# Spatial half's norm summed over one addend, and the first weight's three loads issued by ScalarE's queue

## The chip, the cores and the metric

The kernel runs on one core of a Trainium2 chip. Its engines, as the profile names them, are PE (TensorE: matmuls, with PEld for the loading of the stationary operand), DVE (VectorE), ACT (ScalarE), POOL (GpSimd) and SP (SyncE, which here only issues loads and stores). Each engine works through its own instructions in their written order and waits on semaphores for the others. Loads and stores are moved by 16 DMA engines; an instruction on SP, ACT or POOL issues one, and the transfer then runs beside the engines.

The metric is the device time of one execution in microseconds (us). The kernel before took 1024.92 us, the median of three runs (1023.53 to 1025.2).

## The reference

One decoder layer on 512 tokens of 1024 features, in float32: a SwiGLU feed-forward block, a mixing sub-layer, a second SwiGLU block, a gated per-layer embedding and a last norm. The change touches the embedding's product, which the kernel computes first, and the norm of the mixing sub-layer's spatial half:

```
def rmsnorm(x, g):
    xf = x.astype(jnp.float32)
    y = xf * lax.rsqrt(jnp.mean(xf * xf, axis=-1, keepdims=True) + EPS)
    return (y * g.astype(jnp.float32)).astype(x.dtype)

        ya = chunked_spatial_gating(jax.nn.gelu(u, approximate=False), jax.nn.gelu(v, approximate=False),
                                    gm_ln_g[i], gm_ln_b[i], gm_w_s[i], gm_b_s[i])
        ya = rmsnorm(ya, gm_out_norm[i])
        yb = mamba2_mixer(z, xbc, dt_raw, conv_w[i], conv_b[i], dt_bias[i], a_log[i], d_skip[i], ssm_norm[i])
        h = h + jnp.concatenate([ya, yb], axis=-1) @ w_out[i]
    ...
        gate = jax.nn.sigmoid(rmsnorm(h, ple_norm[i]) @ ple_w_gate[i] + ple_b_gate[i])
        h = h + gate * (p[i] @ ple_w_proj[i])
```

## The kernel before, in words

Features lie on the 128 partitions and tokens along a row, so a tile of 128 features by 512 tokens is the unit of work. Every large product is made of three matmuls: each factor is split into a rounded high part (`hi`, a cast by ACT) and a remainder (`lo`, a subtraction by DVE), and `hi*hi`, `hi*lo` and `lo*hi` are added up in an accumulator bank. So each weight that arrives by DMA passes ACT and then DVE before PE can use it whole.

The program is a list of steps, each with a product on PE, a load, a split and follow-up work. A planner (`run`) issues the steps' parts in turn. For the first steps, up to step 14, the order is written out by hand in the table `ENTRY` (tokens such as `load0`, `split0`, `product0`). The order on PE, ACT, DVE and SP is the written one.

**The entry.** Step 0 is `embedding(0)` (L1187 to L1244 of the kernel before). Its `load` (L1199 to L1203) issues on SP, in this order: the first half of the embedding `p` into the tile `g`; the first weight `ple_proj[0]` into a `raw` tile, in three pieces of 256, 256 and 512 columns (L1202); and the second half of `p` (L1203). Behind them on SP come the second weight `ple_proj[1]` (512 KB, L512), the vector of gains `vec`, the first four tiles of the activations `h` (L1269), the feed-forward weights (`raw`, `rawb`, L512), and the rows of x for the first norm (`whix`, `wlox`, L384). A load waits for an earlier load on the same semaphore, and there are eight of these, used in turn; so from the eighth load or so each one waits for an earlier one to have landed. The split of step 0 (L1215 to L1221) casts the first half of `p` and the first two pieces on ACT and DVE, and then the second half of `p` with the third piece. Its product (L1231) is 24 matmuls of 512 columns, first twelve from the first half and then twelve from the second.

Before that product, PE runs seven matmuls on zeros (L174), and ACT runs one copy of a single column (L175), whose only use is that ACT's function table is loaded there.

**The spatial half's norm.** In the mixing sub-layer the eight tiles `u[i]` are multiplied by their gates on DVE (L1833, `mix_times_u`). For the norm over all features the squares are needed, summed over tiles and partitions. An object `gn` of the class `Norm` squares the first seven tiles on ACT and adds them on POOL into one tile, `ssum` (L276 to L280). The eighth square (L1838) is kept apart in `mix["sq"]`, a tile called `tmp`. The method `sums` (L299 to L311) then sums over partitions with matmuls of one column against a tile of ones (L307): for each of four chunks of 128 tokens one with `ssum` and one with the last square, both into the same column. PE does this behind the product of the second output step (`out_steps[1].rest`); DVE then forms the factor per token (L240 to L246), spreads it over a diagonal (L331), and PE multiplies that by ones (L344).

## Time and profile before

| | us |
|---|---|
| median of three runs | 1024.92 |
| the profiled execution | 1026.13 |
| its span, first to last instruction | 1024.1 |
| PE busy in the span | 1009.1 |
| DVE busy | 843.8 |
| ACT busy | 581.0 |
| first matmul of the embedding starts at | 4.97 |
| second weight `ple_proj[1]` lands at | 9.41 |
| spatial half's norm: its first matmul of one column starts at | 574.73 |

A row of the timeline gives start and duration in us, the engine, the line, the operation with output and inputs, the shapes, a count, and in brackets the idle time ahead of it and what ended it. A row of the chain of waits gives start, duration and what the end of the program waited for in that time. A row of the table by stretches gives, for each engine, its busy time and in brackets its instructions, then the granted clock of PE, the mean busy share of the 16 DMA engines, and what they moved in GB/s. The granted clock of PE was 0.995 over the span.

### The profile page before, as it was taken

How to read it: one execution, taken by the hardware profiler on the slowest of the kernel's cores; microseconds unless marked ns; L12 is line 12 of the kernel's file. 1: busy time of each engine (PE TensorE's matmuls, PEld its weight loads, DVE VectorE, ACT ScalarE, POOL GpSimd, SP SyncE). 2: the span in 40 equal slices, each digit the busy share in tenths (PEclk: the TensorE clock that was granted, in tenths of full speed). 3: DMA queues.
4: the chain of work that ended last, by engine and by line, in shares of the span. 5: the costliest groups of instructions: out<-in, count | busy, mean ns of one | idle time of the engine just before them, and what ended most of it. 6: DMA issues, size and time to landing. Idle time of an engine off the chain costs nothing.

```text
span 1024.1 us, 18334 instructions
## 1 busy us (share of the span) xinstructions
PE 1009.1 (99%) x7472; PEld 951.9 (93%) x7472; DVE 843.8 (82%) x1111; ACT 581.0 (57%) x781; POOL 134.1 (13%) x141
## 2 busy tenths in 40 slices
PE   9999999999999999999999999999999999999996
PEld 7899999999999799888888888899999999999996
DVE  6988888879988797776998757778888888988985
ACT  6755545457667374575754434455445456666745
POOL 0101001002311000144333000101010000330101
PEclk9999999999999999999999999999999999999998
DMA  8977678649962233454432334837677656994412
GB/s 337 325 206 198 192 206 197 195 149 226 207 160 73 82 116 97 148 154 131 137 111 83 103 103 142 215 116 190 183 213 204 176 167 209 217 207 141 136 62 83
DMA packets 51188, 168.89 MB, mean 165 GB/s; under 512 B 5792, under 2 KB 6304, under 8 KB 51104
## 3 DMA queue, kind: packets, MB, share of 16 engines
q1 hardware_dynamic: 39440, 125.71, 36.3%
q0 software_dynamic: 11520, 41.95, 22.1%
q8 instruction: 58, 0.95, 0.4%
q14 instruction: 26, 0.21, 0.1%
q10 hardware_dynamic: 144, 0.07, 0.0%
HBM read 163.44 MB, written 4.26 MB: 164 GB/s over the span
## 4 chain that ended last, share of the span: by engine, by line
PE 85%; DVE 8%; DMA 3%; ACT 2%; issue 1%; SPq 0%; ACTq 0%; DVEq 0%
PE mm L754 20%; PE a L754 15%; PE a L1140 8%; PE sm L217 6%; PE mm L231 6%; PE mm L1140 5%; PE sm L1140 5%; PE mm L217 5%; PE a L217 4%; PE sm L231 3%; PE a L231 3%; DVE wlo L542 2%; DMA s<-in_ffn_gu 1%; PE sm L848 1%; DMA wlox<-in_x_rows 1%
## 5 line engine op out<-in xcount | busy, mean ns | idle before, releaser
L542 DVE TENSOR_TENSOR wlo<-raw,whi 128x1024 fp32r<-128x1024 f32 (+2 forms) x162 | 199.3, 1231 | 66.0 <-ACT whi L538 65.8
L538 ACT CAST whi<-raw 128x1024 fp32r<-128x1024 f32 (+2 forms) x162 | 166.3, 1032 | 139.8 <-DVE raw L764 30.9
L754 PE MATMUL mm<-xfb,whi 128*128 128x256 f32 x960 | 163.9, 275 | 0.0
L754 PEld LDWEIGHTS mm<-xfb,whi 128*128 128x128 f32 x960 | 145.9, 192 | 0.0
L754 PE MATMUL mm<-xfb,wlo 128*128 128x256 f32 x480 | 132.1, 275 | 0.6 <-DVE wlo L542 0.6
L538 ACT CAST whi<-rawb 128x1024 fp32r<-128x1024 f32 x76 | 79.7, 1049 | 62.8 <-DVE rawb L764 29.5
L542 DVE TENSOR_TENSOR wlo<-rawb,whi 128x1024 fp32r<-128x1024 f32 x76 | 92.7, 1220 | 21.3 <-ACT whi L538 20.5
L754 PE MATMUL a<-xfb,whi 128*128 128x256 f32 x640 | 109.4, 275 | 0.0
L754 PEld LDWEIGHTS a<-xfb,whi 128*128 128x128 f32 x640 | 97.3, 192 | 0.0
L754 PEld LDWEIGHTS mm<-xfb,wlo 128*128 128x128 f32 x480 | 92.2, 192 | 0.8 <-DVE wlo L542 0.8
L754 PE MATMUL a<-xfb,wlo 128*128 128x256 f32 x320 | 88.1, 275 | 0.0
L1140 PE MATMUL a<-xfb,whi 128*128 128x256 f32 x480 | 80.7, 275 | 0.0
L1140 PEld LDWEIGHTS a<-xfb,whi 128*128 128x128 f32 x480 | 72.8, 192 | 0.0
L769 POOL DMA_DIRECT2D raw<-in_ffn_gu x20 | 17.2, 862 | 401.7 <-DVE G L916 116.9
L217 PE MATMUL sm<-x,whi 128*128 128x512 f32 x224 | 69.7, 393 | 0.0
L1140 PE MATMUL a<-xfb,wlo 128*128 128x256 f32 x240 | 66.0, 275 | 0.0
L912 ACT ACTIVATE G<-G 128x512 f32<-128x512 f32 x40 | 25.3, 634 | 66.5 <-DVE G L910 65.3
L754 PEld LDWEIGHTS a<-xfb,wlo 128*128 128x128 f32 x320 | 61.4, 192 | 0.1
L754 PE MATMUL a<-xfa,whi 128*128 128x256 f32 x320 | 54.7, 275 | 0.1
L754 PE MATMUL mm<-xfa,whi 128*128 128x256 f32 x320 | 54.8, 275 | 0.0
L1140 PE MATMUL mm<-xfb,whi 128*128 128x256 f32 x320 | 53.8, 275 | 0.0
L1140 PE MATMUL sm<-xfb,whi 128*128 128x256 f32 x320 | 53.8, 275 | 0.0
(430 smaller groups left out, 2612.9 us busy)
## 6 DMA issues: line engine op xcount, KB each, us to landing
raw<-in_ffn_gu SPq DMA_DIRECT2D x56, 512.0 KB, 5.0
rawb<-in_ffn_gu SPq DMA_DIRECT2D x32, 512.0 KB, 8.5
raw<-in_w_in SPq DMA_DIRECT2D x28, 512.0 KB, 3.6
s<-in_ffn_gu SPq DMA_DIRECT2D x20, 512.0 KB, 5.6
raw<-in_ffn_gu POOLq DMA_DIRECT2D x20, 512.0 KB, 6.0
s<-in_ffn_gu POOLq DMA_DIRECT2D x20, 512.0 KB, 9.5
rawb<-in_ffn_dw POOLq DMA_DIRECT2D x18, 512.0 KB, 8.1
raw<-in_w_out SPq DMA_DIRECT2D x16, 512.0 KB, 3.3
```

Of the source, the lines that this page charges most:

```text
L217: nc.tensor.matmul(ps, w, turned(x), start=first and n == 0, stop=last and n == 2, skip_group_check=True)
L231: nc.tensor.matmul(ps[:, tok], wt[:, c], turned(xt[:, tok]), start=first and k == i == 0, stop=last and k == len(xs) - 1 and i == len(by_p ...
L538: nc.scalar.copy(self.hi[:, c], self.raw[:, c])
L542: nc.vector.tensor_tensor(self.lo[:, c], self.raw[:, c], self.hi[:, c].bitcast(F32), ALU.subtract)
L754: nc.tensor.matmul(o, wt[:, c], turned(xt), start=fresh and p == m == n == 0, stop=last and n == 2, skip_group_check=True,)
L769: nc.gpsimd.dma_start(w21.raw, self.src[0], accum_op=ALU.add)
L848: nc.tensor.matmul(ps, (whi, whi, wlo)[n][:, c], t[:, 0:2, n % 2].rearrange("p s (b i) -> p s i b", b=2), start=not lower and p == n == 0, ...
L912: nc.scalar.activation(t, t, AF.Silu)
L1140: nc.tensor.matmul(o, wt[:, c], xt, start=i in (1, 7) and t == jj == n == d % 2 == 0, stop=t == nt - 1 and jj == 1 and d % 2 == 1 and n == ...
```

## The change: what it does

There are two independent parts.

1. The three pieces of the first weight are issued on ACT's queue instead of SP's. ACT's one-column copy, and with it the table load, is moved from ahead of everything to behind these three issues.
2. The eighth square of the spatial half's norm is added to the total by DVE. `sums` loses its second addend, so four matmuls of one column remain where there were eight.

```
-    nc.scalar.copy(vec_warm, ones[:, 0:1])
...
-        def sums(self, more=None):
+        def sums(self):
 
             t = self.totals[0]
             for other in self.totals[1:]:
                 nc.vector.tensor_tensor(t, t, other, ALU.add)
             ps = sm_ps()
             for c in range(NC):
-                for part in (t,) if more is None else (t, more):
-                    nc.tensor.matmul(
-                        ps[:, c : c + 1], part[:, c * P : (c + 1) * P], ones[:, 0:1],
-                        start=part is t, stop=part is not t or more is None,
-                    )
+                nc.tensor.matmul(
+                    ps[:, c : c + 1], t[:, c * P : (c + 1) * P], ones[:, 0:1], start=True, stop=True
+                )
             return ps
...
             for c in halves + (slice(T, 2 * T),):
-                nc.sync.dma_start(w.raw[:, c], a["ple_proj"][q][:, c])
+                nc.scalar.dma_start(w.raw[:, c], a["ple_proj"][q][:, c])
             nc.sync.dma_start(raw[:, 1], a["p"][:, 1])
+            nc.scalar.copy(vec_warm, ones[:, 0:1])
...
         nc.vector.tensor_tensor(u[i], u[i], mix["t", i], ALU.mult)
-        if i < ND - 1:
-            gn.add(u[i])
-        else:
-            mix["sq"] = tmp()
-            nc.scalar.activation(mix["sq"], u[i], AF.Square)
+        if i == ND - 1:
+            gn.engines = (nc.vector,)
+        gn.add(u[i])
...
-    out_steps[1].rest = lambda: gm.update(ps=gn.sums(mix["sq"]))
+    out_steps[1].rest = lambda: gm.update(ps=gn.sums())
```

What stands on the engines is shown at two places. First the start of SP, before; `g` is the embedding's tile, `raw_120` the first weight, `raw_125` the second, `vec` the gains, `h` the activations:

```order
1 L1199 DMA g_98<-in_p 128x512
2 L1202 DMA raw_120<-in_ple_proj 128x256 x2
3 L1202 DMA raw_120<-in_ple_proj 128x512
4 L1203 DMA g_98<-in_p 128x512
5 L512 DMA raw_125<-in_ple_proj 128x1024
6 L1197 DMA vec_69<-in_vecs 128x180
7 L1269 DMA h_94<-in_x 128x512 x2
```

And SP now (line numbers are those of the changed kernel):

```order
1 L1196 DMA g_97<-in_p 128x512
2 L1200 DMA g_97<-in_p 128x512
3 L509 DMA raw_125<-in_ple_proj 128x1024
4 L1194 DMA vec_69<-in_vecs 128x180
5 L1267 DMA h_93<-in_x 128x512 x2
6 L1267 DMA h_94<-in_x 128x512 x2
```

Everything on SP behind the first load stands three issues further forward. The same place on ACT, before; `ghi` and `whi` are the casts of `p` and of the first weight:

```order
1 L175 ACT_TABLE_LOAD
2 L175 COPY warm_75<-ones_76 128x1
3 L1215 CAST ghi_144<-g_98 128x512
4 L1217 CAST whi_146<-raw_120 128x256
5 L1217 CAST whi_146<-raw_120 128x512
```

And ACT now:

```order
1 L1199 DMA raw_119<-in_ple_proj 128x256 x2
2 L1199 DMA raw_119<-in_ple_proj 128x512
3 L1201 ACT_TABLE_LOAD
4 L1201 COPY warm_75<-ones_76 128x1
5 L1213 CAST ghi_144<-g_97 128x512
6 L1215 CAST whi_146<-raw_119 128x256
```

The three issues stand ahead of the table load; the casts keep their order. The second place is DVE at the last tile of the spatial half, before; `u` is the tile, `wlo` the remainder of an output weight, `nv` the first instruction of the norm's factor:

```order
612 L542 TENSOR_TENSOR wlo_6247<-raw_5962,whi_6246 128x1024
613 L1833 TENSOR_TENSOR u_6241<-u_6241,tmp_6244 128x512
614 L542 TENSOR_TENSOR wlo_6281<-raw_6026,whi_6280 128x1024
615 L542 TENSOR_TENSOR wlo_6321<-raw_6102,whi_6320 128x1024
616 L240 TENSOR_SCALAR nv_6325<-sm_6284 128x4
```

And DVE now:

```order
612 L539 TENSOR_TENSOR wlo_6247<-raw_5962,whi_6246 128x1024
613 L1831 TENSOR_TENSOR u_6241<-u_6241,tmp_6244 128x512
614 L279 TENSOR_TENSOR ssum_5950<-ssum_5950,tmp_6251 128x512
615 L539 TENSOR_TENSOR wlo_6282<-raw_6026,whi_6281 128x1024
616 L539 TENSOR_TENSOR wlo_6318<-raw_6102,whi_6317 128x1024
```

The addition into `ssum` stands between the gating of the last tile and the remainders of two output weights; on PE the pairs of L307 (`ssum`, then `tmp`) become four matmuls with `ssum` alone.

## The prediction

> **What bounds the kernel now.** I read the page first, then the chain of waits of the first 60 us, PE's own waits in the timeline, and last the stretch around the spatial half's norm.

> ```profile
> span 1024.1 us, 18334 instructions
> PE 1009.1 (99%) x7472; PEld 951.9 (93%) x7472; DVE 843.8 (82%) x1111; ACT 581.0 (57%) x781; POOL 134.1 (13%) x141
> ```

> PE is busy for 1009.1 of 1024.1 us. So two things can shorten the program: taking work off PE, or filling the few holes in it. The change tries one of each. The holes that matter to its first part are all in the entry:

> ```profile
> 8.69 0.92 PE L1231 MATMUL sm<-ghi,whi 128*128 128x512 f32 x3 [0.33 <-ACT ghi L1219]
> ...
> 27.64 0.70 PE L848 MATMUL sm<-xfb,whi 128*128 128x512 f32 x2 [0.46 <-ACT whi L538]
> 28.89 0.48 PE L848 MATMUL sm<-xfb,wlo 128*128 128x512 f32 x1 [0.56 <-DVE wlo L542]
> 45.75 0.38 PE L754 MATMUL mm<-xfb,wlo 128*128 128x256 f32 x1 [0.61 <-DVE wlo L542]
> ```

> Four stalls, 0.33 + 0.46 + 0.56 + 0.61 = 1.96 us. The chain of waits says what is behind the last of them:

> ```profile
> 0.81 0.38 SPq L1199
> ...
> 1.25 0.42 SPq L1202
> ...
> 1.72 0.42 SPq L1202
> ...
> 2.19 0.43 SPq L1202
> ...
> 2.66 0.43 SPq L1203
> ...
> 3.13 6.28 DMA raw<-in_ple_proj
> ...
> 9.43 6.19 DMA h<-in_x
> ...
> 15.63 9.84 DMA wlox<-in_x_rows
> ...
> 33.18 10.67 DMA s<-in_ffn_gu
> ...
> 45.75 2.72 PE mm L754 x22
> ```

> Up to 45.75 us the end of the program does not hang on PE but on SP's queue: five issues, then the second weight's load (3.13 to 9.41), then a load of `h` that waits for it, then one of the norm's rows, some work of ACT and DVE, and a load of `s`. From 45.75 on the chain is PE's own work. A shift of this chain therefore moves the end of the program, as long as PE's work ahead of 45.75 can move with it, and that has the 1.96 us of stalls to give up.

> **Part 1: three issues leave SP.** The second weight's issue stands at 3.13. The three issues at L1202 take from 1.25 to 2.66, so without them it goes out 2.66 - 1.25 = 1.41 us sooner, at 1.72. That is the upper end for a shift by issue alone. Whether the landings follow is another question, since the load took 6.28 us where loads of this size elsewhere land sooner:

> ```profile
> raw<-in_w_in SPq DMA_DIRECT2D x28, 512.0 KB, 3.6
> ```

> Much of the 6.28 us is spent behind the loads ahead of it. The table by stretches shows how full the 16 DMA engines were:

> ```profile
> 2.00:5.00 3.00, 3.00 (x8) 1.87 (x7) 0.43 (x2) 1.02 (x4) 0.00 (x0) 1.00 0.85 270
> 5.00:7.00 2.00, 2.00 (x8) 1.71 (x8) 1.15 (x2) 0.91 (x2) 0.00 (x0) 1.00 0.58 184
> 7.00:8.00 1.00, 1.00 (x7) 0.85 (x5) 0.00 (x0) 0.00 (x0) 0.00 (x0) 1.00 0.97 349
> 8.00:46.00 38.00, 36.04 (x188) 30.95 (x187) 34.17 (x56) 29.33 (x43) 1.92 (x2) 1.00 1.04 380
> ```

> From 8 to 46 us they are full: nothing can be gained there, but whatever is moved earlier is passed on unchanged, because the same bytes then end earlier. Before 8 us they were idle for 3 x 0.15 + 2 x 0.42 + 0.03 = 1.3 us. So two different bounds agree: 1.41 us of issue, 1.3 us of idle DMA time. The lower bound is zero: from 5 to 7 us the engines were only 0.58 busy although the second weight had been issued at 3.13, so something besides the issue held the loads back, and that may stay. A second queue gives the engines other loads to take up meanwhile. I take 1.0 us, about three quarters of the idle time, nearer to the upper bounds because both the issue and the overlap of queues work the same way; for the likeliest case I allow 0.5 to 1.2.

> [...]

> What does ACT pay? Its rows at the start, and the only load or store that it issues in this program:

> ```profile
> 0.81 1.28 ACT L175 ACT_TABLE_LOAD   x1 [0.81 <-PEq L2177]
> 1.66 3.35 PE L174 MATMUL sm<-tmp 128*128 128x512 f32 x7 [1.66 <-DVE tmp L171]
> 4.21 0.62 ACT L1215 CAST ghi<-g 128x512 fp32r<-128x512 f32 x1 [1.92 <-DMA g<-in_p]
> 4.97 1.44 PE L1231 MATMUL sm<-ghi,whi 128*128 128x512 f32 x3
> 6.19 0.63 ACT L1217 CAST whi<-raw 128x512 fp32r<-128x512 f32 x1 [0.91 <-DMA raw<-in_ple_proj]
> 8.01 0.62 ACT L1219 CAST ghi<-g 128x512 fp32r<-128x512 f32 x1 [1.20 <-DMA g<-in_p]
> ...
> 394.12 0.67 ACTq L1497 DMA_DIRECT2D cs_dram<-csrow  x1
> ```

> ACT is free from the table load's end (2.09, and a copy of 0.2) until the first half of `p` lands at 4.21. Three issues at SP's price (0.43 and a gap of 0.04 each) end at 2.2, the table load then at 3.5, the copy at 3.7: hidden. At ACT's own price of 0.67 they end at 2.9, the table load at 4.2, the copy at 4.4: the first cast is 0.2 us late. Queued behind it are the casts for the first twelve matmuls; PE waits for them, but PE is held by its seven matmuls on zeros until 5.0 in any case, and it has the stall at 8.69 to make up for a late start. That stall ends sooner, since the second half of `p` (cast at 8.01) is issued 1.41 us earlier. The pieces themselves go out at 0.81, 1.5 and 2.2 by ACT's price, against 1.25, 1.72 and 2.19: none is later. I book nothing for ACT; without the cover it is 0.2 us of the 1.96.

> [...]

> **Part 2: four matmuls less, one addition more.** The rows around the norm, then the row for additions of this shape on DVE:

> ```profile
> 542.55 1.05 PE L307 MATMUL sm<-ones,ssum 128*128 128x1 f32 x8
> 543.47 1.14 PE L1819 MATMUL a<-xs,ya 128*128 128x128 f32 x8
> ...
> 568.93 1.27 POOL L280 TENSOR_TENSOR ssum<-ssum,tmp 128x512 f32<-128x512 f32 x1 [5.41 <-ACT tmp L279]
> 571.51 0.68 DVE L1833 TENSOR_TENSOR u<-u,tmp 128x512 f32<-128x512 f32 x1
> 572.28 0.63 ACT L1838 ACTIVATE tmp<-u 128x512 f32<-128x512 f32 x1 [1.95 <-DVE u L1833]
> 573.88 1.23 DVE L542 TENSOR_TENSOR wlo<-raw,whi 128x1024 fp32r<-128x1024 f32 x1 [1.69 <-ACT whi L538]
> 574.73 0.28 PE L307 MATMUL sm<-ones,ssum 128*128 128x1 f32 x2
> 576.43 0.68 PE L231 MATMUL mm<-yb,whi 128*128 128x512 f32 x2
> 576.98 0.15 DVE L240 TENSOR_SCALAR nv<-sm 128x4 f32<-128x4 f32 x1
> 579.42 1.29 DVE L331 TENSOR_TENSOR tmp<-ident,tokp 128x512 fp32r<-128x512 f32 x2
> 581.70 0.63 PE L344 MATMUL sm<-tmp,onesr 128*128 128x512 f32 x2
> ...
> L280 DVE TENSOR_TENSOR ssum<-ssum,tmp x7: 683/684/686, 618.8 to 655.0; 128x512 f32<-128x512 f32 x7
> ```

> Eight matmuls take 576.43 - 574.73 = 1.70 us on PE; four, in another norm, 543.47 - 542.55 = 0.92. PE has no hole here, so the saving of 1.70 - 0.92 = 0.78, or half of 1.70 = 0.85, is on the path: I take 0.8.

> The addition is 0.68 us on DVE. The square ends at 572.91 and POOL's last addition at 570.20, so it can run from about 572.95 to 573.65. DVE was idle from 572.2 to 573.88, waiting for a cast. So neither the addition nor its new wait delays the remainder at 573.88, which is what stands behind it and what PE needs for the next product. PE's first matmul at 574.73 finds the total 1.1 us old. If the square came 0.25 us later, the remainder would be late, with a further 1 us of cover on PE. What is late next: the next product ends 0.8 sooner, so the spread at 581.70 moves to 580.9, while its input (DVE's second diagonal, done at 580.71, set by the remainders ahead of `nv` and not by the sums) stays. That leaves 0.2 us: nothing lost, up to 0.1 if a semaphore is slow.

> **Sum.** 1.0 + 0.8 = 1.8 us. The profiled execution took 1026.13 with a span of 1024.1, and the runs' median is 1024.92, 1.2 below it; the difference lies outside what the change touches, so I take the 1.8 from the span (1022.3) and from the median alike: 1024.92 - 1.8 = 1023.1.

> **Rivals.**
> *The transfers set the pace.* The second weight lands near 9.4 whenever it is issued. For it: DMA engines not full from 5 to 7 us with the load already issued. Against it: they were idle for 1.3 us, and a second queue can use that. Shift 0 to 0.5; at 0.2 the time is 1024.92 - 0.8 - 0.2 = 1023.9.
> *The full shift.* All 1.41 us arrive, or up to 1.7 because the two queues also hide each other's slow packets; PE's 1.96 us allow that. For it: the two agreeing bounds. Against it: the 0.58. Time 1024.92 - 0.8 - 1.4 = 1022.7.
> *ACT starts late.* The table load waits until ACT's three loads have landed. The third piece was there at 6.19; then 1.28, the copy 0.2 and the cast 0.62 put the first matmul at 8.4, 3.4 us late. PE can give up 1.96, the rest, 1.4, is lost, less the 0.8: 1025.6, slower than before. It decides from a first matmul later than 4.97 + 1.96 + 0.8 = 7.7. Against it: nothing in the program makes the table load wait for those loads, and no row shows ACT held after its own issue.

> **How the numbers follow.** Likeliest case 0.49 (1022.9 to 1023.6), transfers 0.25, full shift 0.21, ACT late 0.05. What a measurement of this kernel can tell from no change is about 0.2%, 2.05 us, so faster begins at 1022.87. That takes the full shift (0.21), and with half a microsecond between medians about 0.14 of the likeliest case: 0.35. Slower by as much needs the late ACT and more: 0.04. The rest, 0.61, is the same. The range reaches from the full shift with 1.7 us and a fast median (1022.3) to no shift at all, 1024.1, with 0.7 us more, a little under half of the spread of the runs shown (1023.53 to 1025.2): 1024.8.

> **What would show it.** Right: the second weight's issue near 1.72 and its landing near 8.4; the stall at 8.69 gone; the last stall's matmul at 44.7 instead of 45.75; four matmuls at L305 taking 0.9 us; DVE's addition ending before the remainder's cast is done; spread and everything after 1.8 us sooner. Wrong: a landing still at 9.4, a first matmul after 5.5, or a new wait of PE between 574 and 582.

## The result, and the profile after

| | before | after |
|---|---|---|
| median, us | 1024.44 (8 executions, 1023.09 to 1025.73) | 1021.7 (8 executions, 1019.99 to 1023.26) |
| ratio | | 0.9977, 95% interval 0.9968 to 0.9986 |
| profiled execution, us | 1026.13 | 1021.68 |
| its span, us | 1024.1 | 1019.8 |
| granted clock of its span | 0.995 | 0.999 |

The change is faster by 2.7 us in the median, 0.23% by the ratio and so just over what the prediction took as the border of no change. That is more than the 1.8 of the prediction's sum, and lies below its range (1022.3 to 1024.8). In the two profiled executions the difference is 4.45 us, so the first question is where it lies. For this I took matmuls that are the same in both programs and subtracted their starts in the timelines:

| matmul that starts before at | after, us later (+) or sooner (-) |
|---|---|
| 4.97 (first product) | +0.52 |
| 8.69 (thirteenth matmul) | +2.26 |
| 45.75 | -0.16 |
| 78.21 | -0.27 |
| 339 | -0.17 |
| 348.2 | -1.87 |
| 560 | -1.88 |
| 581.70 (spread of the norm) | -2.78 |
| 1005.1 | -2.79 |
| 1010 | -4.42 |

Three things happened, and only one of them looks as it was booked. The norm gives 0.90 us at its place. The entry gives 0.2 to 0.3, not 1.0. And two steps of 1.7 and 1.6 us come at 342 and 1006 us, where the change edits nothing.

**The norm.** Timeline of the changed kernel around the norm; rows as in the part before:

```profile
567.05 1.27 POOL L279 TENSOR_TENSOR ssum<-ssum,tmp 128x512 f32<-128x512 f32 x1 [5.43 <-ACT tmp L278]
...
571.13 0.69 DVE L279 TENSOR_TENSOR ssum<-ssum,tmp 128x512 f32<-128x512 f32 x1 [0.83 <-ACT tmp L278]
...
572.00 1.23 DVE L539 TENSOR_TENSOR wlo<-raw,whi 128x1024 fp32r<-128x1024 f32 x1 [0.17 <-ACT whi L535]
...
572.84 0.95 PE L305 MATMUL sm<-ones,ssum 128*128 128x1 f32 x8
...
578.92 0.63 PE L341 MATMUL sm<-tmp,onesr 128*128 128x512 f32 x2
```

DVE's addition (0.69) ends at 571.82, before ACT's cast lets the remainder start at 572.00, and PE's four matmuls take 0.95 and wait for nothing. The spread has no bracket: no wait took the place of the saving.

**The entry.** Timeline of the changed kernel, ACT and then PE:

```profile
0.80 1.38 ACTq L1199 DMA_DIRECT2D raw<-in_ple_proj  x3
2.21 1.28 ACT L1201 ACT_TABLE_LOAD   x1 [2.21 <-issue]
3.50 0.19 ACT L1201 COPY warm<-ones 128x1 f32<-128x1 f32 x1
4.83 0.62 ACT L1213 CAST ghi<-g 128x512 fp32r<-128x512 f32 x1 [1.13 <-DMA g<-in_p]
...
1.66 3.36 PE L174 MATMUL sm<-tmp 128*128 128x512 f32 x7 [1.66 <-DVE tmp L171]
5.50 1.81 PE L1229 MATMUL sm<-ghi,whi 128*128 128x512 f32 x3 [0.48 <-ACT ghi L1213]
7.10 0.63 PE L1229 MATMUL a<-ghi,whi 128*128 128x512 f32 x1
7.53 1.49 PE L1229 MATMUL sm<-glo,whi 128*128 128x512 f32 x3
...
10.51 0.63 PE L1229 MATMUL a<-ghi,wlo 128*128 128x512 f32 x1
10.94 0.96 PE L1229 MATMUL sm<-ghi,whi 128*128 128x512 f32 x3
11.74 0.38 PE L1229 MATMUL a<-ghi,whi 128*128 128x512 f32 x1
```

ACT issues at 0.46 us each and is done with the copy at 3.69, as the cheaper of the two prices had it. But the first half of `p` lands later: its cast starts at 4.83 instead of 4.21. The second and third piece of the weight are later too, though their issues were not: their casts start at 6.06 and 8.08 instead of 4.87 and 6.19. So PE has a hole of 0.48 us at 5.02. And behind it a single matmul of 512 columns takes 0.63 until 10.9 us, where the kernel before had 0.38 from 6.25 on: the starts are 0.43 apart instead of 0.215, half speed. The first twelve matmuls take 5.4 us, where they took 3.2 before (4.97 to 8.2). The kernel after can afford that, since its loads run ahead. The table by stretches of the changed kernel (columns as before):

```profile
2.00:5.00 3.00, 3.00 (x7) 1.81 (x6) 0.00 (x0) 1.65 (x3) 0.00 (x0) 1.00 0.96 268
5.00:7.00 2.00, 1.51 (x4) 0.99 (x4) 1.49 (x3) 0.85 (x2) 0.00 (x0) 1.00 1.04 405
7.00:8.00 1.00, 1.00 (x4) 0.73 (x4) 0.18 (x1) 0.00 (x0) 0.00 (x0) 1.00 1.07 395
```

The DMA engines' shares are 0.96, 1.04 and 1.07 where they were 0.85, 0.58 and 0.97: the idle time is used up. The clock column says 1.00 although PE is at half speed: the clock records begin at 11.2 us in this trace and at 6.1 in that of before, about where the matmuls' starts come closer together (from 0.43 to 0.215 apart here), and up to there only that spacing tells the speed. The chain of waits of the changed kernel begins

```profile
0.80 4.00 DMA g<-in_p
...
5.50 1.81 PE sm L1229 x3
...
7.74 1.28 PE sm L1229 x3
```

and stays on PE from there up to 225 us: the four stalls of 1.96 us are gone, and PE itself is late.

**The steps at 342 and 1006 us.** PE has two holes (waits) there in both programs, each ahead of the one-column matmuls that sum a norm's squares. PE's timeline, kernel before and then the kernel after:

```profile
342.51 1.05 PE L307 MATMUL sm<-ones,ssum 128*128 128x1 f32 x8 [1.92 <-DVE ssum L296]
...
1004.18 0.61 PE L1992 MATMUL sm<-ones,sq 128*128 128x1 f32 x4 [1.52 <-ACT sq L1977]
```

```profile
342.33 1.05 PE L305 MATMUL sm<-ones,ssum 128*128 128x1 f32 x8 [1.91 <-DVE ssum L295]
...
1001.39 0.61 PE L1988 MATMUL sm<-ones,sq 128*128 128x1 f32 x4 [1.54 <-ACT sq L1973]
```

The holes are the same. What differs is the clock behind them. The table by stretches, kernel before:

```profile
342.00:344.00 2.00, 1.49 (x11) 1.44 (x12) 1.92 (x4) 0.00 (x0) 0.00 (x0) 1.00 0.04 13
344.00:346.00 2.00, 2.00 (x7) 1.55 (x6) 1.65 (x11) 0.00 (x0) 0.00 (x0) 0.51 0.54 161
346.00:348.00 2.00, 2.00 (x8) 1.65 (x6) 1.34 (x3) 0.00 (x0) 0.00 (x0) 0.64 0.02 7
...
1006.00:1008.00 2.00, 2.00 (x13) 2.00 (x12) 0.43 (x1) 1.51 (x4) 1.42 (x8) 0.55 0.00 0
1008.00:1010.00 2.00, 2.00 (x13) 2.00 (x12) 0.41 (x2) 0.32 (x1) 0.95 (x5) 0.59 0.00 0
```

and the kernel after:

```profile
344.00:346.00 2.00, 2.00 (x11) 1.76 (x10) 1.68 (x11) 0.00 (x0) 0.00 (x0) 1.00 0.61 164
346.00:348.00 2.00, 2.00 (x11) 1.76 (x10) 1.16 (x2) 0.00 (x0) 0.00 (x0) 1.00 0.01 4
...
1006.00:1008.00 2.00, 2.00 (x21) 2.00 (x20) 1.24 (x5) 1.04 (x3) 0.58 (x3) 1.00 0.00 0
1008.00:1010.00 2.00, 2.00 (x20) 1.82 (x17) 1.67 (x5) 1.99 (x5) 0.00 (x0) 1.00 0.00 0
```

The columns are those of the table above: behind POOL stand the granted clock, the DMA share and GB/s. Before, the clock was 0.5 for 3.41 us behind each hole (about 344.0 to 347.4, and 1006.2 to 1009.6), and PE did 7 matmuls in 2 us instead of 11. Half of 3.41 is 1.7 us lost, twice. In the profile after, the clock stays full in both places. The two stretches of half clock have one length, 3.413 us in the clock records, and start 194.0 of these lengths apart (344.03 and 1006.22). The holes ahead of them are shorter than that: 1.9 and 1.5 us, each followed by about 0.9 us of one-column matmuls.

So the theory to test (**clock theory**): the change itself is worth about 0.9 at the norm and somewhat more than 0.3 in the entry; the rest is stretches of half clock (**half-clock windows**, 3.41 us long, 1.7 us lost in each) that executions of the changed kernel have less often. The rival (**shift theory**): the loads' shift and the norm make the whole gain, and this pair of traces had an unlucky entry after and an unlucky clock before.

### The profile page after: what moved, and what is told of

It is laid out like the page before. It is cut to its first block, busy times and chain, and to the rows that moved or that the text cites. A ratio compares the mean times of both kernels' runs of the same rounds, so it can differ in the third digit from the quotient of the medians.

```text
span 1019.8 us, 18319 instructions
## 1 busy us (share of the span) xinstructions
PE 1006.1 (99%) x7464; PEld 949.8 (93%) x7464; DVE 844.5 (83%) x1112; ACT 581.0 (57%) x781; POOL 134.2 (13%) x141
## 4 chain that ended last, share of the span: by engine, by line
PE 88%; DVE 6%; ACT 2%; issue 1%; DMA 1%; SPq 0%; ACTq 0%; DVEq 0%
PE mm L751 21%; PE a L751 15%; PE a L1137 8%; PE sm L216 6%; PE mm L230 6%; PE mm L1137 5%; PE sm L1137 5%; PE mm L216 5%; PE a L216 4%; PE sm L230 3%; PE a L230 3%; PE sm L845 2%; DVE wlo L539 2%; PE a L845 1%; PE mm L845 1%
## 6 DMA issues: line engine op xcount, KB each, us to landing
raw<-in_ffn_gu SPq DMA_DIRECT2D x56, 512.0 KB, 5.1
rawb<-in_ffn_gu SPq DMA_DIRECT2D x32, 512.0 KB, 8.4
raw<-in_w_in SPq DMA_DIRECT2D x28, 512.0 KB, 3.6
s<-in_ffn_gu SPq DMA_DIRECT2D x20, 512.0 KB, 5.8
raw<-in_ffn_gu POOLq DMA_DIRECT2D x20, 512.0 KB, 6.9
s<-in_ffn_gu POOLq DMA_DIRECT2D x20, 512.0 KB, 9.9
rawb<-in_ffn_dw POOLq DMA_DIRECT2D x18, 512.0 KB, 8.0
raw<-in_w_out SPq DMA_DIRECT2D x16, 512.0 KB, 3.2
```

## The experiments

Medians, with the kernel before run beside them each time; over all runs of this study the kernel before had 130 executions with a median of 1024.6 (1022.66 to 1027.06).

### Filling the two holes

Idle matmuls of 128 columns into the bank that the sums will use next, queued on PE ahead of the sums, so that PE is busy while it waits:

```
+    def busy(ps, n):
+        for _ in range(n):
+            nc.tensor.matmul(ps[:, :P], ones_r, ones_r, start=True, stop=True)
...
             ps = sm_ps()
+            busy(ps, fill)
...
-    behind_product(1, mix_steps[0].late, lambda: mix.update(ps=mix_norm.sums()))
+    behind_product(1, mix_steps[0].late, lambda: mix.update(ps=mix_norm.sums(fill=24)))
...
         ps = ple["sums", tok.start]
+        if first and not tok.start:
+            busy(ps, 20)
```

The first is the norm at 342 us, the second the last norm, at 1002. What the idle matmuls write is overwritten by the sums.

> The kernel before, with 24 idle matmuls of 128 columns put into PE's 1.9 us hole at 342 us and 20 into its 1.5 us hole at 1002 us; they end before the sums that PE waits for arrive. Clock theory: the trace of before shows PE at half clock for 3.41 us behind each of these two holes (344 to 347.4 and 1006.1 to 1009.5, 1.7 us lost each), the trace after shows none; so a good part of the gain is these windows, and filled holes take them away from the kernel before too: no half clock behind either hole, median 1022.3 to 1023.0 instead of 1024.4. Shift theory: all of the gain is the moved loads (1.7 us) and the norm (0.9 us); the holes matter little, median 1024.4, within 0.4.

Measured: 1022.93 (1022.35 to 1024.79), ratio 0.9983 (0.9975 to 0.9992). The clock theory's number, 1.9 us below the kernel before (1024.83 beside it); no half clock behind either hole in the profile (granted clock 0.999 over its span).

> The changed kernel with the same idle matmuls in both holes. Clock theory: what the change gives by itself is the norm's 0.9 us and 0.3 to 1.3 us of the entry, so this stands 1.2 to 2.2 us below the kernel before with filled holes: 1020.7 to 1021.5, a little below the changed kernel's 1021.7, and with less spread. Shift theory: 2.6 us below the kernel before with filled holes, 1021.7 like the changed kernel.

Measured: 1022.1 (1021.01 to 1022.82). Neither: 0.8 below the kernel before in the same form, less than both theories said, and above the changed kernel itself. One reason is the price of the idle matmuls, in the timeline of this run:

```profile
340.23 2.79 PE L157 MATMUL sm<-onesr 128*128 128x128 f32 x24
342.86 1.00 PE L310 MATMUL sm<-ones,ssum 128*128 128x1 f32 x8
```

24 of them take 2.63 us, 0.11 each, longer than the hole: the sums start 0.5 us late, and 0.45 at the second hole.

### Closing the hole at 5 us

```
-WARM = 7
+WARM = 9
```

> The changed kernel with nine matmuls on zeros ahead of the first product instead of seven, so that PE has no hole of 0.48 us at 5.02. Clock theory: PE is at full clock from 5.1 to 8.5 us instead of 10.9, the first twelve matmuls take 2.6 to 4.3 us instead of 5.4, and everything up to 340 us lies 1.0 to 1.5 us earlier; the holes at 342 and 1002 can still cost 1.7 us each, so the median is 1020.0 to 1022.0. Shift theory (loads set the entry's pace, PE has slack): 1021.7, within 0.4, and the work at 340 us stays where it is.

Measured: 1021.83, in groups: 1020.16, 1020.17, 1020.6; then 1021.83, 1021.92, 1021.99; then 1023.66. The groups are one half-clock window (1.7 us) apart. The profile is that of the slowest execution, and has both windows; its entry has the full clock from 7.2 us, and the matmul of 78.21 comes 1.45 us sooner than before. So with the full clock early, the loads' shift reaches PE.

> Nine matmuls on zeros and both holes filled, on the changed kernel. Clock theory: no half clock left after 8.5 us: 1019.8 to 1020.4, the fastest of the four, with executions within 0.5 us of each other. Shift theory: 1021.7, within 0.4.

Measured: 1021.25 (1021.07 to 1022.93): above the expected 1020.4, by about the 0.95 us that the idle matmuls cost here too. The executions did not stay within 0.5 us of each other: two of seven lie at 1022.67 and 1022.93.

The same with fewer idle matmuls:

```
-            busy(ps, 20)
+            busy(ps, 11)
...
-mix_norm.sums(fill=24)
+mix_norm.sums(fill=15)
```

> Nine matmuls on zeros at the start and both holes filled, with 15 and 11 idle matmuls instead of 24 and 20: each takes 0.11 us, so 24 took 2.6 us and ended 0.5 us too late, and 20 took 2.2 and ended 0.45 too late, while 15 take 1.65 and 11 take 1.2 and end inside the holes of 1.9 and 1.5. Clock theory: 0.9 us below the one with 24 and 20 (1021.25): 1020.2 to 1020.5, no half clock behind the holes, the fastest so far. If idle matmuls must reach to the end of a hole to hold the clock, windows of half clock come back and the median is 1021 to 1022.

Measured: 1020.15, and all five executions between 1020.11 and 1020.23: ratio 0.9957 (0.9945 to 0.9969). This is the fastest kernel of the study. Its timeline at the two holes:

```profile
338.88 1.79 PE L157 MATMUL sm<-onesr 128*128 128x128 f32 x15
340.95 1.05 PE L310 MATMUL sm<-ones,ssum 128*128 128x1 f32 x8 [0.29 <-DVE ssum L299]
...
998.26 1.34 PE L157 MATMUL sm<-onesr 128*128 128x128 f32 x11
999.96 0.61 PE L1995 MATMUL sm<-ones,sq 128*128 128x1 f32 x4 [0.36 <-ACT sq L1978]
```

0.29 and 0.36 us of the holes are left, so nothing is delayed, and the clock stays up: behind the first hole matmuls of 512 columns start 0.22 us apart (342.38 and 342.60), behind the second those of 256 columns 0.11 (1001.18 and 1001.29).

### Each part alone, and the change a second time

Part 1 alone is the change without its lines on the norm; of the change's diff this remains:

```
-    nc.scalar.copy(vec_warm, ones[:, 0:1])
...
-                nc.sync.dma_start(w.raw[:, c], a["ple_proj"][q][:, c])
+                nc.scalar.dma_start(w.raw[:, c], a["ple_proj"][q][:, c])
             nc.sync.dma_start(raw[:, 1], a["p"][:, 1])
+            nc.scalar.copy(vec_warm, ones[:, 0:1])
```

Part 2 alone is all the rest of that diff, with loads and copy as before.

> Part 1 alone: the three loads on ACT's queue and the table load behind them; the norm as before. Clock theory: the loads of the second weight and of all behind it move forward by 0.75 to 1.8 us, but PE has its hole of 0.5 us at 5.0 and stays at half clock until 8.9 to 12.3 us, so the work at 68 us lies only 0.3 us earlier (1.3 earlier to 0.4 later, by where the clock's window of 3.41 us happens to lie). The hole at 1002 then lies 660.4 us behind the hole at 340, 193.5 windows, and falls into one window as a whole more often than with both parts: median 1023.4 to 1024.8, 0 to 1.4 us below the kernel before. Shift theory: 1.7 us below the kernel before, 1023.1.

Measured: 1024.06 (1022.91 to 1025.98), ratio 0.9995 (0.9987 to 1.0004): inside the clock theory's range, and not told from no change. Its profile is of the slowest execution, with half clock behind both holes; its entry has the full clock from 6.4 us, and the work at 78.21 comes 1.77 us sooner, at 76.44.

> Part 2 alone: the last square added by DVE, four sums instead of eight; the loads as before. Both theories: the matmuls behind the norm start 0.9 us earlier, nothing waits anew. Clock theory: half-clock windows behind the holes at 342 and 1002 come as often as in the kernel before, so the median is 0.9 us below it, within 0.5 (about 1023.9), with executions in groups 1.7 us apart. Shift theory: 0.9 us below, the same.

Measured: 1022.67 (1020.82 to 1024.51), ratio 0.9982 (0.9974 to 0.9991): 2.15 us below the kernel before beside it, more than twice the four matmuls and more than either theory said. A small, steady share of it lies outside the span: time minus span is 2.08 us on average in the kernel before (122 executions) and 2.09 in part 1 alone, but 1.86 here and 1.85 in the changed kernel. These 0.23 us come with part 2; no trace covers that time, so their cause stays open.

> The changed kernel once more, for a second trace and more executions. Clock theory: again a first matmul at 5.4 to 5.9, half clock until 8.9 to 12.3, and mostly no half clock behind 342 and 1002 us, since PE's work from 5.5 on has no wait that is not its own and so follows the moment at which the clock rises: median 1021.2 to 1021.9, more than the 0.3 + 0.9 us of the two parts below the kernel before. Shift theory: the entry's 1.7 us are to be seen at 68 us in this trace, since the first trace was an unlucky one.

Measured: 1020.69 (six executions, 1020.05 to 1023.44), below the expected range; with the eight of the first run 1021.44. The expectation for the entry was wrong, and this is the shift theory's point. Its timeline:

```profile
1.66 3.35 PE L174 MATMUL sm<-tmp 128*128 128x512 f32 x7 [1.66 <-DVE tmp L171]
5.49 1.49 PE L1229 MATMUL sm<-ghi,whi 128*128 128x512 f32 x3 [0.47 <-ACT ghi L1213]
6.82 0.38 PE L1229 MATMUL a<-ghi,whi 128*128 128x512 f32 x1
...
9.22 0.92 PE L1229 MATMUL sm<-ghi,whi 128*128 128x512 f32 x3 [0.30 <-ACT ghi L1217]
```

The same hole (0.47), and yet the full clock from 6.4 us on by the clock records. The work at 78.21 then comes 1.68 us sooner, at 76.53. So behind nearly the same hole at 5 us (0.48 and 0.47) two executions of one kernel had the full clock at 11.2 and at 6.4 us.

### The parts with the holes filled

The same four kernels with 15 and 11 idle matmuls in the holes, so that only the parts differ.

> The kernel before with both holes filled by 15 and 11 idle matmuls, which end inside the holes. Clock theory: 0.95 us below the one with 24 and 20 (1022.93), 1021.7 to 1022.3, and the groups 1.7 us apart are gone: this is the kernel before without half clock behind 342 and 1002, 2.8 us below the kernel before. If the holes' half clock costs less than that, 1023 or more.

> Part 1 alone with both holes filled: what the moved loads are worth without the holes' half clock. Clock theory: 1.7 us below the kernel before with filled holes when the clock is full by 8.5 us (traces of part 1 alone and of the changed kernel's second profile, -1.78 and -1.68 at 68 us), 0.3 us when it stays half until 11 (the changed kernel's first profile): two groups, median 0.3 to 1.7 below. Against it: 0, if part 1 is worth nothing as the run of part 1 alone (1024.06) suggests.

> Part 2 alone with both holes filled. Clock theory: part 2 itself is worth 0.9 us (eight matmuls to four), the other 1.2 us of the 2.15 us that part 2 alone gave came from fewer half-clock windows and vanish here: 0.9 us below the kernel before with filled holes, within 0.3. If part 2 moves more than the four matmuls, 2 us.

> The changed kernel with both holes filled (seven matmuls on zeros). Clock theory: two groups, 1020.1 (full clock by 8.5 us) and about 1021.5 (half clock until 11), 1.2 to 2.6 us below the kernel before with filled holes: the sum of the two parts, with no gain of their combination.

And with nine matmuls on zeros as well:

> The kernel before with nine matmuls on zeros and both holes filled (15 and 11). Its entry hangs on the loads and not on PE, so two more matmuls on zeros change little: 1022.4 as with seven, within 0.5. If nine matmuls by themselves are worth something: 1021.5.

> Part 2 alone in the same form: 0.9 to 1.0 below the run of the kernel before in this form, about 1021.4. What then lies between this and the changed kernel in this form (1020.15) is part 1 without its hole: 1.0 to 1.7 if the loads' shift is worth what the traces show, 0 to 0.3 if the medians of the runs with seven matmuls are right.

Measured, medians in us:

| | neither part | part 1 | part 2 | both |
|---|---|---|---|---|
| as they are | 1024.6 | 1024.06 | 1022.67 | 1021.44 |
| holes filled | 1022.37 | 1022.35 | 1021.33 | 1021.30 |
| holes filled, nine matmuls on zeros | 1022.23 | | 1021.51 | 1020.15 |

Read down the columns: half clock behind the two holes costs the kernel before 2.3 us, part 1 alone 1.7, part 2 alone 1.3, the changed kernel 0.1. Medians of executions that fall into groups jump from one group to the next, so the means are the surer guide: 1.9, 1.7, 1.0 and 0.4. Read across the second row: without that, the change is worth 1.1 us (means: 1022.59 and 1020.97, 1.6), nearly all of it part 2's 1.0; part 1 adds nothing in the median and 0.3 to 0.7 in the mean. So the expectations for e9 and e11 came about right, and the gains expected of e10 and e12 did not come in full in the median. Nor did e9's spread vanish: it runs from 1021.51 to 1024.0, in part outside the span (its profiled execution took 1024.0 with a span of 1020.7). Across the third row, with the hole at 5 us closed as well: part 1 is worth 1.36 and part 2 0.72. In this form some executions of the two kernels without part 1 still had a half-clock window (1022.5 and more; the profile of e18 shows one at 343.1, so the idle matmuls do not always hold the clock); among those that lie below, the medians are 1021.9, 1021.17 and 1020.15, so that part 2 is worth 0.7 and part 1 1.0.

The entries agree with it. Over all profiles the 48 matmuls of the row at 78.21 start at 77.16 to 78.21 with the entry as before (eight profiles, mean 77.66), at 76.44 to 76.76 with part 1 and the full clock by 7.2 us (seven, mean 76.58), and at 77.80 to 77.94 with part 1 and half clock until 11 (the first profile of the change, e2 and e10). Two lie apart: e13 at 76.99 with the full clock from 9.2 us, and e14 at 78.75 with its added work. So part 1 is worth about 1.1 us with the clock, and nothing without it.

### Why fewer windows

That leaves 2.2 us (2.3 - 0.1) by the medians that the change gives by avoiding half clock, though it edits neither hole. By the means it is 1.5 (1.9 - 0.4), with a standard error of 0.5 from the spread of the executions. The granted clock, which every execution reports, says roughly how many windows there were: each takes 3.413 x 0.5 / 1022 = 0.00167 off the mean clock of the same kernel with filled holes (e9 to e12).

| | mean clock | holes filled | windows |
|---|---|---|---|
| before (the 122 run beside experiments) | 0.9963 | 0.9985 | 1.3 |
| part 1 alone | 0.9963 | 0.9984 | 1.3 |
| part 2 alone | 0.9973 | 0.9984 | 0.7 |
| both (14 executions) | 0.9979 | 0.9990 | 0.7 |

The count is rough, since every profile also has half clock at the program's end, for 1.2 to 4.3 us (4.2 in the profile before, 1.7 in the profile after), and the mean clock counts that too. By this count part 2 is what halves them, and one thing that it changes is the distance between the holes: 660.4 us from the start of one to the start of the other when the first brings no half clock, which is 193.46 windows, against 659.4 or 193.19. Three theories were put to the test: the distance between the holes decides (D), the place of both holes in the raster on which the half-clock windows lie (194.0 lengths apart in the profile before) decides (P), or it was chance which executions were caught (C). Three runs move the holes by idle matmuls in front of a norm's spread, at 579 us (between the holes) or at 39.6 (ahead of both):

```
-        def spread(diags, ps=None, by=lambda t: t):
+        def spread(diags, ps=None, by=lambda t: t, delay=0):
             ps = sm_ps() if ps is None else ps
+            busy(ps, delay)
...
-    out_steps[2].rest = lambda: gn.spread(gm["diags"], gm["ps"])
+    out_steps[2].rest = lambda: gn.spread(gm["diags"], gm["ps"], delay=8)
```

The last two lines are those of e13; in e15 it is 23, and in e14 the 8 stand at the first spread of the program.

> The changed kernel with eight idle matmuls (0.11 us each, 0.88 in all) on PE at 579 us, between the two holes: the holes then lie 660.3 us apart, 193.45 windows of 3.413 us, as in the kernel before. Theory D: the windows of half clock come back, on average one per execution as before instead of 0.25, so the time rises by 0.9 + 1.3 to 1023.6, 1022.9 to 1024.3. Theories P and C: by 0.9 to 1022.3.

> The changed kernel with the same eight idle matmuls at 39.6 us, ahead of both holes: the distance between them stays 193.19 windows. Theories D and C: the time rises by 0.9 to 1022.3. Theory P: the holes leave their safe place and the time rises by 1.7 to 3 us, 1023.1 to 1024.4.

> The kernel before with 23 idle matmuls (2.5 us) between the holes: 662.9 us apart, 194.2 windows, as in the changed kernel but for one whole window. Theory D: the half-clock windows halve, from one per execution to 0.5, so the 2.5 us of extra work cost only 1.6: 1026.3, 1025.7 to 1026.7. Theories P and C: 2.5 us, 1027.2.

In the next table the windows are counted as in the last one, and the mean of e15 is set against that of the kernel before beside it.

| | median | mean, against that of its own kernel | mean clock | windows |
|---|---|---|---|---|
| e13, between, +0.84 us of work | 1023.21 | +1.9 | 0.9970 | 1.2 |
| e14, ahead, +0.84 | 1023.51 | +1.9 | 0.9976 | 0.9 |
| e15, between, +2.5 on the kernel before | 1026.53 | +2.1 | 0.9973 | 0.7 |

The medians of e13 and e15 lie in the ranges of theory D, that of e14 in the range of theory P. By the means, 0.84 us of idle matmuls cost 1.9 at either place, 1.1 more than their work (standard error 0.3). So chance alone (theory C) does not explain it, but these times do not show the distance to be the cause either. e15 decides nothing: the kernel before beside it had a median of 1023.88 and a mean of 1024.30, and the interval of the ratio, 1.0 to 3.2 us, holds both D's 1.6 and the full 2.5.

The traces say more. In e13's profile the first hole passes and the second one is caught:

```profile
344.00:346.00 2.00, 2.00 (x11) 1.00 0.29 109
...
1002.00:1004.00 2.00, 2.00 (x14) 0.62 0.00 0
1004.00:1006.00 2.00, 2.00 (x11) 0.52 0.00 0
```

(columns: PE alone, then clock, DMA share, GB/s). Over the ten profiles without filled holes, the second one was caught in three of three with a distance of about 193.46 windows (as it is without half clock behind the first), and in two of seven with about 193.2 or 194.2; one of these two is e14, whose distance was kept.

What separates them is the place of a hole in the raster of windows. Each trace gives this raster by the times at which its clock changed: in all eight profiles with such windows, they start a whole number of window lengths behind the clock's first rise (in the profile before 99.0 and 293.0 lengths behind the rise at 6.11 us). Take a hole together with the 0.9 to 1.6 us of one-column matmuls behind it, and of this the longest part that lies within one window. Of the twenty holes in these ten profiles, the ten that brought half clock have 1.95 to 2.80 us there (2.80 and 2.30 in the profile before); the others have 1.24 to 1.91, and one 1.96 (1.90 and 1.24 in the profile after). The three profiles of the changed kernel (after, e7 and e16) lie just below this border, with 1.82 to 1.96 at the first hole and 1.24 to 1.32 at the second. In e14 everything is a quarter of a window later, and the second hole has 2.06. So e14 is no exception: in these profiles half clock goes with the place of each hole, and the distance counts since it sets the place of the second one.

That half clock goes with the place is read from these ten profiles; how the other executions lie was not seen, and that the place is the cause was not shown. So it is likely, but not shown, that the change has fewer windows because its two holes lie better.

### What makes `p` late

```
             nc.sync.dma_start(raw[:, 1], a["p"][:, 1])
-            nc.scalar.copy(vec_warm, ones[:, 0:1])
...
     for _ in range(WARM):
         nc.tensor.matmul(ps, idle[:, :P], idle, start=True, stop=True)
+    nc.scalar.copy(vec_warm, ones[:, 0:1])
```

> The changed kernel with ACT's copy where it was: the program then issues the first piece on ACT, loads the table, and issues the second and third piece 1.5 us later. If the first half of p lands later because it shares the DMA engines with all three pieces, it lands sooner here: its cast starts at 4.2 to 4.6 instead of 4.83, the hole of PE at 5 us shrinks to 0.2 or less, but the third and fourth matmul then wait for the second piece. If it is something else, the cast stays at 4.83.

Measured: 1020.2 us in a single execution. ACT's timeline:

```profile
0.82 0.41 ACTq L1200 DMA_DIRECT2D raw<-in_ple_proj  x1
1.26 1.28 ACT L175 ACT_TABLE_LOAD   x1 [1.26 <-PEq L2173]
1.32 0.87 ACTq L1200 DMA_DIRECT2D raw<-in_ple_proj  x2
2.56 0.19 ACT L175 COPY warm<-ones 128x1 f32<-128x1 f32 x1
4.77 0.62 ACT L1213 CAST ghi<-g 128x512 fp32r<-128x512 f32 x1 [2.02 <-DMA g<-in_p]
```

The edit did not do what the expectation supposed: the second and third issue went out at 1.32, while the table was being loaded. So the loads were at the engines as early as in the changed kernel, and `p` was as late (4.77). The place of the table load is indifferent here, and the run did not separate the causes. The packets in the traces do show the sharing: until the first half of `p` was moved, at 3.91 us, ACT's queue had moved 110 KB in the first profile of the change (104 KB in e16). At the 268 GB/s of that stretch this is an estimated 0.4 us of the 0.6; the rest stays open.

## Why the prediction was wrong

Point by point, against the steps of the prediction.

- *Second weight's issue at 1.72*: 1.71. *Landing near 8.4*: 7.8 (6.1 us after its issue). Right, and better than booked. *The stall at 8.69 gone*: only where PE itself is late; with the clock early (e7) it is still there, 0.30 us at 9.22.
- *ACT pays nothing*: its own work fitted as the sum had it (0.46 per issue, copy done at 3.69, predicted 3.7). But the first half of `p` came 0.6 us later. The sum had no term for that. For the pieces of the weight it reckoned only with their issues ("none is later"); the casts of the second and third started 1.2 and 1.9 us later. The first matmul came at 5.50, on the edge of its own mark for wrong.
- *Part 1 is worth 1.0*: with the full clock early it is 1.1 in the profiles and 1.0 to 1.4 in the medians with nine matmuls on zeros, so the term was right. As the kernel stands part 1 gives 0.5, not told from nothing: behind the hole at 5 us (0.42 to 0.82 us) the clock stays low in some profiles, in the first one for 2 us of PE time, which eats what the loads gain.
- *Part 2 is worth 0.8*: 0.90 in the two traces, 0.7 to 1.0 in the medians with filled holes; the addition's cover and the spread's slack were as described. Right, but for the 0.23 us outside the span, which no term had.
- *The sum*: 1.8, against 2.7 to 3.2 measured. The step that failed is the one that carries it to the median: "the difference lies outside what the change touches, so I take the 1.8 from the span (1022.3) and from the median alike". That sum takes PE's rows at the speed at which they stand, and assumes that what the change leaves alone stays as long as it was. It does not: about 2 us of the kernel before (1.9 by the means, 2.3 by the medians) are half clock behind two holes, and the change takes 1.5 of it away (2.2 by the medians). Even the 1.2 us between the profiled execution and the median fit this, as an estimate: two windows in the profile against 1.3 on average, 0.7 x 1.7. Neither the sum nor a rival had a term for the clock; it stood at nothing. Why the holes are caught less often is shown for single profiles only (their place in the raster).
- The row for it was at hand. The granted clock of the span was 0.995, not 1; the table by stretches shows 0.51 and 0.55 behind the two longest of PE's waits later on. The prediction used it only up to 46 us.
- *Rivals*: the full shift (1022.7) was nearest, but by luck: the loads gave 1.1 with the clock and nothing without it, not 1.4. That two queues hide each other's slow packets, from which the upper 1.7 us of this rival and the lower end of the range come, no run shows; with nine matmuls on zeros and filled holes part 1 gave 1.0 to 1.4. The transfers did not set the pace, and ACT did not wait for its loads.

## What to carry to other kernels

Where one engine is busy for 99% of the span, look at its clock behind each of its longest holes before an edit is priced: a hole of 1.5 us that costs 1.5 us can cost another 1.7 behind it (here the one at 1002 us, in the profile before), in some executions and not in others, and a change far away can move that. Executions that fall into groups 1.7 us apart (as in e3) are the sign. A few idle matmuls that end before the awaited data arrives mostly held the clock here: 15 and 11 of them, with two more at the start, took the changed kernel to 1020.15 us and its spread from 3.4 to 0.1 (five executions).
